# Sums of u in the FFN's first down product, and sums of weights by SP's and POOL's queues

## Chip, cores and metric

The kernel runs on 1 core of one Trainium2 chip. The metric is the device time of one execution in microseconds, the median of three runs. A profile of one execution shows what each engine did: PE (TensorE, matmul) with PEld (its weight loads), DVE (VectorE), ACT (ScalarE), POOL (GpSimd) and SP (SyncE, which here only issues transfers). "Lnnn" is a line of the kernel of the profile.

## What is computed

Two layers of a decoder trunk over 528 positions (16 learned meta tokens and a sequence of 512) with 1024 channels. Each layer has a mixer (attention with forget gates, a Conformer convolution module and a short gated convolution, side by side) and a gated FFN:

```python
def ffn_sublayer(h, pre_g, post_g, w_up, conv_w, w_down):
    u = rms_norm(h, pre_g)
    z = jnp.einsum("bld,df->blf", u, w_up)
    z = causal_depthwise_conv(z, conv_w)          # 3 taps
    g, up = jnp.split(z, 2, axis=-1)
    y = jnp.einsum("blf,fd->bld", jax.nn.silu(g) * up, w_down)
    return h + rms_norm(y, post_g)
```

D_FF is 2816, so there are 22 blocks of 128 gate rows and 22 of up rows. All is float32.

## The kernel before

**Tiling.** Activations lie transposed: 128 channels of a k block on the partitions, 8 such blocks (KD), 528 columns. Weights are laid out by the host in chunks, mostly 128 x 1024 floats (512 KB): one block of output rows with all eight k blocks. A float32 product is made of three matmuls on two-part numbers: every weight chunk is loaded into a `raw` buffer (three of them) by SP, cast by ScalarE into `whi` (L579, L569, L716) and subtracted by VectorE into `wlo` (L580, L570, L720); activations are split alike (`uhi`, `ulo`; `y` for the FFN's gated rows, L2111 and L2112). `mm3` (L764) makes hi x hi, hi x lo and lo x hi.

**FFN.** The 22 blocks run in three parts of 8, 7 and 7 (PARTS). In each part, every block makes a gate and an up product, scales it (L2060), convolves it by three taps (ScalarE L2092, VectorE L2094 twice), applies SiLU and the product (L2104, L2108), and splits it into `y` (L2111, L2112). Then comes that part's down product, over 8 row blocks of output m: 24 matmuls of 512 columns each, the first two row blocks together with the last k of both held to the end. The part's output is copied (part 0, ScalarE L2323) or added (part 1, VectorE L2325) into `yp`. The third part's down product is the stage's end.

**Pairs by seven products.** In layer 1, 12 of the blocks after the first part (SEVEN) use a Strassen-like scheme (`seven_pair`, products L2216): gate and up are the two rows of a 2 x 2 block matrix, the halves of k and of the columns make the rest, and seven half-size products replace eight. It needs two things. First, sums of u: `normalised()` writes u times its gain into `yp` (16 steps `un`, L2149), makes four sums in two halves of k (`total` L2168, `split` L2172 and L2173: 8 steps each), and splits u itself into `uhi` and `ulo` (`block`, L2160 and L2161: four steps, each over a half of k and a half of the columns). Second, sums of the weights: for each of the 12 blocks four tiles of 128 x 512 (U0+U1, U0+G0, U0+U1+G0 and all four of U0, U1, G0, G1, the halves of k of up and gate), in two DRAM tensors `w_sum_c` and `w_sum_b`, later loaded as chunks "c" and "b" beside the plain half "d" (L562).

**Where that work stands.** From block 2 of layer 1's first part on, `build(6)` does up to six steps of `normalised()` after each block's product with SiLU; a `None` in the sequence ends a call; after the last block `build()` does all that is left, ahead of the down product. The sums of weights are made by POOL alone: four plain copies and four accumulating transfers of 256 KB per block, in five steps. `tick` takes steps from a list: it copies one element on POOL, which waits for a row of the work (L2129), and issues the step behind it (L531). Six blocks are done in layer 0's FFN, one step a tick, and six in layer 1's first part, two steps a tick.

**What sets the order.** In the mixers and around the ends of the down products a planner (`Flow`) writes out the order of PE, ACT, DVE and POOL. Everywhere else, and on SP's queue throughout, the order is fixed when the program is built: what is ready and finds its engine free is put next, the earliest in the program first. `tc.issue_after(ins)` puts those instructions of a block that run on the engine of `ins` behind it, and no others. SP issues one transfer at a time and waits in order. In the mixers, `flow.op("sp", ...)` hands a transfer to the planner; its place in the program is then the planner's, but SP is not among the engines whose order is written out.

At the start, SP loads `pv`, the first weights (L712) and h (L492), and then weights as `raw` buffers come free.

## Time and profile before

| | us |
|---|---|
| median of 3 runs (1287.41 to 1289.52) | 1288.8 |
| the profiled execution | 1289.34 |
| its span, first to last instruction | 1287.5 |
| VectorE busy | 888.6 |
| ScalarE busy | 667.1 |
| POOL busy | 201.0 |

The transfers that the change touches, from the profile's list of issues (line, engine, operation, count, size of each, median time from issue to landing):

```profile
w_sum_c<-in_w_dram POOLq DMA_DIRECT2D x36, 256.0 KB, 5.7
w_sum_b<-in_w_dram POOLq DMA_DIRECT2D x36, 256.0 KB, 6.4
raw<-w_sum_c SPq DMA_DIRECT2D x12, 512.0 KB
raw<-w_sum_b SPq DMA_DIRECT2D x12, 512.0 KB
...
w_sum_b<-w_sum_c POOLq DMA_DIRECT2D x12, 256.0 KB, 5.0
...
w_sum_c<-w_sum_b POOLq DMA_DIRECT2D x12, 256.0 KB, 5.2
```

The span covers the first to the last instruction; the execution's own time is 1.84 us longer. A wait is written as "engine, target, line <- releaser"; in a timeline each row has its start, its length, the engine, the line, and in brackets the idle time before it with what ended it. Busy shares of PE are modelled, since matmuls are pipelined. An idle engine costs time only where another, in the end TensorE, waits for it.

### The profile page before, as it was taken

Reading aid. Unit: us, or ns where it says so; the run is one execution under the profiler, and the core shown is the slowest. Engines: PE = TensorE matmul, PEld = TensorE weight load, DVE = VectorE, ACT = ScalarE, POOL = GpSimd, SP = SyncE. Lnnn points to the kernel's source line nnn. Section 1 sums busy time; section 2 is a strip of 40 time slices with the busy share of each in tenths; the row PEclk is TensorE's granted clock in tenths of the full one; section 3 lists DMA queues with packets and bytes.
Section 4 is the critical chain, followed back from the end, with each engine's and each line's share of the span. In section 5 each row is a group of like instructions: output and inputs, shape, how many; then the busy total and the mean of one; then the engine's idle time right before and its main releaser. Section 6 shows DMA issues by size and latency. Waiting matters only on the chain. (4 is left out here: it accounts for less than half of the span.)

```text
span 1287.5 us, 24257 instructions
## 1 busy us (share of the span) xinstructions
PE 1264.1 (98%) x9660; PEld 1209.6 (94%) x9660; DVE 888.6 (69%) x1505; ACT 667.1 (52%) x1273; POOL 201.0 (16%) x406
## 2 busy tenths in 40 slices
PE   8999999999999999999999999999999899999997
PEld 8999899999999999999999998899999689979997
DVE  7888765688644665576588877756799438746864
ACT  7254577564333333244573545766546347626663
POOL 1313311002132013100003133100043330000000
PEclk9999999999999999999999999999999899999999
DMA  7136132504578447523550361334085785434621
GB/s 240 34 101 159 51 100 96 186 18 158 129 243 257 109 130 238 147 83 94 173 196 18 110 167 39 97 130 151 17 213 149 159 248 181 135 123 135 190 73 66
DMA packets 64305, 171.97 MB, mean 134 GB/s; under 512 B 7920, under 2 KB 18288, under 8 KB 64192
## 3 DMA queue, kind: packets, MB, share of 16 engines
q1 hardware_dynamic: 51664, 138.83, 34.1%
q0 software_dynamic: 12528, 31.59, 10.4%
q8 instruction: 76, 1.25, 0.4%
q14 instruction: 37, 0.30, 0.1%
HBM read 148.93 MB, written 35.78 MB: 143 GB/s over the span
## 5 line engine op out<-in xcount | busy, mean ns | idle before, releaser
L764 PE MATMUL psum<-y,whi 128*128 128x264 f32 (+3 forms) x1968 | 386.4, 300 | 5.7 <-ACT y L2111 2.5
L764 PE MATMUL psum<-uhi,whi 128*128 128x264 f32 (+1 forms) x1456 | 349.0, 288 | 1.8 <-ACT uhi L1990 0.8
L764 PE MATMUL psum<-ulo,whi 128*128 128x264 f32 (+1 forms) x1456 | 343.2, 284 | 0.6 <-DVE ulo L1992 0.4
L764 PE MATMUL psum<-uhi,wlo 128*128 128x264 f32 (+1 forms) x1456 | 342.6, 284 | 0.0
L764 PEld LDWEIGHTS psum<-y,whi 128*128 128x128 f32 x1968 | 305.9, 189 | 21.1 <-ACT y L2111 2.9
L764 PE MATMUL psum<-y,wlo 128*128 128x264 f32 (+3 forms) x984 | 273.9, 298 | 0.6 <-DVE wlo L720 0.6
L764 PEld LDWEIGHTS psum<-uhi,whi 128*128 128x128 f32 x1456 | 245.6, 188 | 6.3 <-issue 2.0
L764 PEld LDWEIGHTS psum<-ulo,whi 128*128 128x128 f32 x1456 | 246.0, 188 | 1.3 <-DVE ulo L1992 0.6
L764 PEld LDWEIGHTS psum<-uhi,wlo 128*128 128x128 f32 x1456 | 245.7, 188 | 0.0
L764 PEld LDWEIGHTS psum<-y,wlo 128*128 128x128 f32 x984 | 177.9, 189 | 6.3 <-DVE wlo L720 1.0
L579 ACT CAST whi<-raw 128x1024 fp32r<-128x1024 f32 (+1 forms) x98 | 100.5, 1028 | 160.5 <-PE psum L764 139.2
L580 DVE TENSOR_TENSOR wlo<-raw,whi 128x1024 fp32r<-128x1024 f32 (+1 forms) x98 | 117.1, 1197 | 61.5 <-ACT whi L579 60.5
L2094 DVE SCALAR_TENSOR_TENSOR c<-zs,pv,c 128x528 f32<-128x528 f32 (+1 forms) x176 | 131.6, 756 | 4.7 <-ACT c L2092 2.7
L720 DVE TENSOR_TENSOR wlo<-raw,whi 128x1024 fp32r<-128x1024 f32 (+2 forms) x80 | 95.5, 1204 | 33.1 <-ACT whi L716 32.5
L716 ACT CAST whi<-raw 128x1024 fp32r<-128x1024 f32 (+2 forms) x80 | 81.8, 1030 | 25.4 <-PE psum L764 17.9
L1080 DVE SCALAR_TENSOR_TENSOR cacc<-apad,pv,cacc 128x528 f32<-128x528 f32 x120 | 87.6, 772 | 0.1
L2092 ACT ACTIVATE c<-zs,pv 128x528 f32<-128x528 f32 (+1 forms) x88 | 63.5, 728 | 10.6 <-DVE zs L2254 7.7
L2129 POOL COPY cols<-y 128x1 f32<-128x1 f32 x21 | 18.3, 869 | 303.6 <-ACT y L2111 303.6
L2057 DVE TENSOR_TENSOR zs<-psum,rz 128x528 f32<-128x528 f32 x40 | 28.3, 708 | 53.1 <-PE psum L764 52.1
L2111 ACT CAST y<-c 128x528 fp32r<-128x528 f32 (+1 forms) x44 | 27.6, 628 | 69.4 <-DVE c L2108 69.3
L1535 POOL TENSOR_SCALAR dm<-ident,mcol 128x128 fp32r<-128x128 f32 (+1 forms) x80 | 33.6, 420 | 128.6 <-DVE mcol L1527 127.4
L2104 ACT ACTIVATE c<-c 128x528 f32<-128x528 f32 (+1 forms) x44 | 28.1, 638 | 46.6 <-DVE c L2094 46.6
(265 smaller groups left out, 2039.3 us busy)
## 6 DMA issues: line engine op xcount, KB each, us to landing
raw<-in_w_dram SPq DMA_DIRECT2D x148, 512.0 KB
raw<-in_w_dram SPq DMA_DIRECT2D x32, 448.0 KB
w_sum_c<-in_w_dram POOLq DMA_DIRECT2D x36, 256.0 KB, 5.7
w_sum_b<-in_w_dram POOLq DMA_DIRECT2D x36, 256.0 KB, 6.4
raw<-w_sum_c SPq DMA_DIRECT2D x12, 512.0 KB
raw<-w_sum_b SPq DMA_DIRECT2D x12, 512.0 KB
h<-in_x_dram SPq DMA_DIRECT2D x16, 264.0 KB
raw<-in_w_dram SPq DMA_DIRECT2D x14, 256.0 KB
```

The source lines that it names most:

```text
L579: nc.scalar.copy(hi[:, :sz], raw[:, :sz])
L580: nc.vector.tensor_sub(lo[:, :sz], raw[:, :sz], hi[:, :sz].bitcast(F32))
L716: nc.scalar.copy(box["hi"][:, :sz], box["raw"][:, :sz])
L720: nc.vector.tensor_sub(lo[:, :sz], box["raw"][:, :sz], box["hi"][:, :sz].bitcast(F32))
L764: nc.tensor.matmul(d, lhsT=w[a][:, k, cols], rhs=rhs(b, k, hf), start=start and i == 0 and p == 0, stop=stop and i == n - 1 and p == 2)
L1080: nc.vector.scalar_tensor_tensor(conv[j], in0=src, in1=conv[j], scalar=col("a_dw_w", CK * j + i), op0=ALU.mult, op1=ALU.add)
L1535: diag.append(gp(0.5, lambda qs=qs, end=end, n=n, b=b: nc.gpsimd.tensor_scalar(dm[:n, qs:end], in0=ident[:n, :n], scalar1=mcol[:n, b:b + 1 ...
L2057: nc.vector.tensor_mul(two(t[:, off:]), srcs[0], two(rz))
L2092: nc.scalar.activation(dst, src[:, 2:2 + 2 * fw], AF.Copy, scale=wtap(2, t))
L2094: nc.vector.scalar_tensor_tensor(dst, in0=src[:, i:i + 2 * fw], scalar=wtap(i, t), in1=dst, op0=ALU.mult, op1=ALU.add)
L2104: silu = nc.scalar.activation(cs[0], cs[0], AF.Silu)
L2111: nc.scalar.copy(ghi, cs[0])
```

## The change

Sums of weights: a block now has one DRAM tensor `w_sum` of four tiles. Three plain copies (256, 256 and 512 KB) fill it on SP's queue, and three accumulating transfers (512, 256 and 256 KB) on POOL finish it: four steps a block in place of five, three adds for four. Eight blocks are done in layer 0's FFN by ticks, one step a tick; four in layer 1's mixer, given to the planner 40 us apart with a low priority; none in layer 1's FFN. The loads of "c" and "b" take every second tile, two pieces of 512 floats a partition. The two halves in "b" have changed places, and so the two products with them in `seven_pair`.

Sums of u: `build(5)` runs in blocks 2 to 6 of the first part, and not in block 7. What is left runs in the first down product, after the matmuls of each row block (or of the first two) and up to the next `None`, ahead of the copy into `yp`; on the engine of `glo_ins` (VectorE's last subtraction for `y`, then ScalarE's last copy) it stands behind that instruction. `block(k)` now takes two k blocks over all columns: block(0) in the first slot; the second half's eight sums and block(2) in that of row block 2; block(4) and block(6) in the next two.

```diff
--- before.py
+++ after.py
@@ -31,7 +31,8 @@
 
 SEVEN = (8, 9, 10, 11, 12, 13, 15, 16, 17, 18, 19, 20)
 SEVEN_IN = (1,)
-SUMS = {1: {0: 6, 1: 6}}
+SUMS = {1: (8, 4)}
+SUM_US, SUM_LAT, SUM_EVERY = 0.9, 5.0, 40.0
 K2 = KD // 2
 SB = K2 * P
 AHEAD = 2
@@ -524,16 +525,25 @@
     def sum_steps(l, f):
 
         gate, up = (flat_w(up_chunk[l, t]) for t in (f, NF + f))
-        c, b = sums[l, f] = [T(dram, [P, 2 * SB], F32, f"w_sum_{n}{l}_{f}") for n in "cb"]
-        x, y = slice(0, SB), slice(SB, 2 * SB)
-
-        def put(to, src, add=False):
-            nc.gpsimd.dma_start(to, src, **({"accum_op": ALU.add} if add else {}))
-
-        return [lambda: put(c[:, x], up[:, x]), lambda: put(b[:, y], up[:, x])], \
-            [lambda: put(b[:, x], gate[:, x]), lambda: put(c[:, y], gate[:, y])], \
-            [lambda: put(c[:, x], up[:, y], True), lambda: put(b[:, y], gate[:, x], True)], \
-            [lambda: put(b[:, x], c[:, x], True)], [lambda: put(c[:, y], b[:, x], True)]
+        t = sums[l, f] = T(dram, [P, 4, SB], F32, f"w_sum{l}_{f}")
+        n, o = P * 2 * SB, offs[up_chunk[l, f]]
+        diag = wflat[o:o + 2 * (n + SB)].rearrange("(e q) -> e q", e=2)[:, :n].rearrange("e (p s) -> p e s", p=P)[:, :, :SB]
+
+        def put(to, src):
+            nc.gpsimd.dma_start(to, src, accum_op=ALU.add)
+
+        def copies():
+            nc.sync.dma_start(t[:, 0], up[:, :SB])
+            nc.sync.dma_start(t[:, 1], up[:, :SB])
+            nc.sync.dma_start(t[:, 2:4], gate.rearrange("p (e s) -> p e s", e=2))
+
+        return copies, lambda: put(t[:, 0:2], diag), lambda: put(t[:, 2], t[:, 1]), lambda: put(t[:, 3], t[:, 2])
+
+    def sums_at(l, place):
+
+        counts = SUMS.get(l, ())
+        n0 = sum(counts[:place])
+        return SEVEN[n0:n0 + counts[place]] if place < len(counts) else ()
 
     pw_place = [None]
 
@@ -553,13 +563,14 @@
             return
         if i in seven_up:
             if not parts:
-                c, b = sums[seven_up[i]]
-                parts.extend((("c", c), ("b", b), ("d", flat_w(i)[:, SB:])))
+                t = sums[seven_up[i]]
+                parts.extend((("c", t[:, 1::2]), ("b", t[:, 0:3:2]), ("d", flat_w(i)[:, SB:])))
             kind, src = parts.popleft()
             wpos[0] += not parts
             raw = T(wp, [P, CHUNK], F32, "raw", 3)
-            sz = src.shape[-1]
-            nc.sync.dma_start(raw[:, :sz], src)
+            sz = SB if kind == "d" else 2 * SB
+            nc.sync.dma_start(raw[:, :sz] if kind == "d" else raw[:, :sz].rearrange("p (e s) -> p e s", e=2),
+                              src)
             if kind == "c":
                 hi, lo = (T(tx[0], [P, 2 * SB], F32R, t) for t in ("chi", "clo"))
             elif kind == "b":
@@ -1769,6 +1780,12 @@
                 early.begin(0, PAIRS[0], *pair)
             if over == {"maxima", "fill", "exponentials"}:
                 early.begin(1, PAIRS[1], *banks["st"].slots)
+
+        for i, f in enumerate(sums_at(l, 1)):
+            copies, *adds = sum_steps(l, f)
+            tok = flow.op("sp", 2.0, copies, (Tok(flow.pe + SUM_EVERY * i),), prio=8, lat=SUM_LAT)
+            for op in adds:
+                tok = gp(SUM_US, op, tok, prio=8, lat=SUM_LAT)
 
         for g in (then("maxima", maxima()), att_norms(), then("exponentials", exponentials()), then("fill", fill())):
             flow.thread(g)
@@ -2109,28 +2126,21 @@
                 slot = next(f - sum(PARTS[:p]) for p in range(len(PARTS)) if f < sum(PARTS[:p + 1]))
                 ghi, glo = (t[:, :2 * fw] for t in y_pair(slot))
                 nc.scalar.copy(ghi, cs[0])
-                nc.vector.tensor_sub(glo, cs[0], ghi.bitcast(F32))
+                glo_ins[0] = nc.vector.tensor_sub(glo, cs[0], ghi.bitcast(F32))
                 return ghi, glo
 
             n7 = 2 * ((L - i0 + 3) // 4)
             h7 = [(i0, i0 + n7), (L - n7, L)]
             late_ups = deque()
             seven = SEVEN if l in SEVEN_IN else ()
-            todo = deque()
-            for to, counts in SUMS.items():
-                n0 = sum(counts[x] for x in counts if x < l)
-                fs = [sum_steps(to, f) for f in SEVEN[n0:n0 + counts.get(l, 0)]]
-                for x, y in zip(fs[::2], fs[1::2]):
-                    todo.extend(step for both in zip(x, y) for step in both)
+            todo = deque(step for to, place in ((l + 1, 0), (l, 2)) for f in sums_at(to, place) for step in sum_steps(to, f))
 
             def tick(src):
 
                 if todo:
                     t = nc.gpsimd.tensor_copy(ticks, src.bitcast(F32))
                     with tc.issue_after(t.ins):
-                        for _ in range(1 + l):
-                            for op in todo.popleft():
-                                op()
+                        todo.popleft()()
 
             def normalised():
 
@@ -2153,10 +2163,8 @@
                     k0, (a, z) = b
                     return yp[:, k0:k0 + K2, a:z]
 
-                def block(b):
-                    k0, (a, z) = b
-                    a += skip * (b in (b12, b22))
-                    c = (slice(None), slice(k0, k0 + K2), slice(a, z))
+                def block(k):
+                    c = (slice(None), slice(k, k + 2), slice(i0, L))
                     nc.scalar.copy(uhi[c], yp[c])
                     nc.vector.tensor_sub(ulo[c], yp[c], uhi[c].bitcast(F32))
 
@@ -2176,6 +2184,10 @@
                     for k in range(K2):
                         yield lambda b=b, k=k: un(b, k)
                 for k in range(0, K2, 2):
+                    if k:
+                        yield None
+                        yield lambda: block(0)
+                        yield None
                     yield lambda: total(2, k, lambda: at(b12), lambda: at(b22))
                     yield lambda: split(2, k)
                     yield lambda: total(0, k, lambda: at(b11), lambda: at(b12))
@@ -2184,30 +2196,25 @@
                     yield lambda: total(3, k, lambda: at(b21), lambda: raw[1])
                     yield lambda: split(1, k)
                     yield lambda: split(3, k)
-                yield None
-                for b in blocks:
-                    yield lambda b=b: block(b)
+                for k in range(2, KD, 2):
+                    yield lambda k=k: block(k)
+                    yield None
                 ts.extend((t[:, 0], t[:, 1]) for t in tiles)
 
-            mul_ins = [None]
+            mul_ins, glo_ins = [None], [None]
             ts, n_seven, primed = [], [0], set()
             building = [None]
 
-            def build(n=None):
-
-                while building[0] is not None and (n is None or n > 0):
-                    try:
-                        op = next(building[0])
-                    except StopIteration:
-                        building[0] = None
+            def build(n):
+
+                for op in building[0]:
+                    if op is None:
                         return
-                    if op is None:
-                        if n is not None:
-                            return
-                        continue
                     op()
-                    if n is not None:
-                        n -= 1
+                    n -= 1
+                    if n == 0:
+                        return
+                building[0] = None
 
             def product(bank, w, k0, rhs, start, stop):
 
@@ -2246,13 +2253,13 @@
                 nc.scalar.copy(tmp, bz)
                 finish_pair()
                 wb = next_w()
-                product(y, wb, 0, t(1), False, False)
+                product(y, wb, K2, t(1), False, False)
                 nc.scalar.copy(gate[:, hi], by[:, skip:])
                 product(x, w, K2, u(K2, h7[0]), False, True)
                 nc.scalar.copy(gate[:, lo], bx)
                 product(z, wc, K2, u(K2, h7[1]), False, True)
                 nc.vector.tensor_sub(gate[:, hi], bz[:, skip:], gate[:, hi])
-                product(y, wb, K2, t(2), False, False)
+                product(y, wb, 0, t(2), False, False)
                 nc.scalar.copy(up[:, hi], by[:, skip:])
                 nc.vector.tensor_sub(up[:, hi], up[:, hi], tmp[:, skip:])
                 wd = next_w()
@@ -2295,12 +2302,10 @@
                             continue
                         scaled(i, [ps[:, :, :H]] if i0 == 0 else [ps[:, hf, :iws[hf]] for hf in range(2)])
                     g[f] = ffn_gate(f)
-                    if building[0] is not None:
+                    if building[0] is not None and f < PARTS[0] - 1:
                         with tc.issue_after(mul_ins[0].ins):
-                            build(6)
+                            build(5)
                 finish_pair()
-                if part == 0:
-                    build()
                 ks = list(range(nf))
                 grhs = lambda b, k, hf, f0=f0: g[f0 + k][b][:, fw * hf:fw * (hf + 1)]
                 if part < len(PARTS) - 1:
@@ -2314,20 +2319,23 @@
                                     mm3({0: ps[:, 0, :2 * fw]}, w, group, lambda b, k, hf, f0=f0: g[f0 + k][b][:, :2 * fw], **where)
                                 else:
                                     mm3({hf: ps[:, hf, :fw] for hf in range(2)}, w, group, grhs, **where)
+                        if building[0] is not None:
+                            with tc.issue_after(glo_ins[0].ins):
+                                build(99)
                         for m, ps in zip(some, tiles):
                             if final:
                                 d, src = yp[:, m, t0:], ps[:, 0, :2 * fw]
                             else:
                                 d, src = two(yp[:, m, t0:]), ps[:, :, :fw]
                             if part == 0:
-                                nc.scalar.copy(d, src)
+                                glo_ins[0] = nc.scalar.copy(d, src)
                             else:
                                 nc.vector.tensor_add(d, d, src)
                             if l == 0 and m % 2:
                                 store_one()
                             tick(yp[:, m, t0:t0 + 1])
                 else:
-                    assert not todo
+                    assert not todo and building[0] is None
                     if seven:
                         pools.pop().close()
                         pools.append(ExitStack())
```

## Prediction

> **What bounds the kernel now.** I read the page first, then TensorE's waits, the timeline of TensorE around the longest of them, the windows by stage, and SP's queue. The page:
>
> ```profile
> span 1287.5 us, 24257 instructions
> ...
> PE 1264.1 (98%) x9660; PEld 1209.6 (94%) x9660; DVE 888.6 (69%) x1505; ACT 667.1 (52%) x1273; POOL 201.0 (16%) x406
> ...
> PEclk9999999999999999999999999999999899999999
> ```
>
> TensorE has work in 98% of the span: 23.4 us of idle are all that an edit can take away, plus what a slow clock costs. One slice of 40 (the 32nd) has a lower granted clock. TensorE's waits (total, times, longest), of the whole run:
>
> ```profile
> PE psum L764 <- ACT y L2111: 2.5, 1, 2.5
> PE psum L2216 <- ACT chi L569: 1.6, 1, 1.6
> ...
> PE psum L2216 <- ACT zs L2256: 0.8, 1, 0.8
> ...
> PE psum L1598 <- POOL pf L1578: 0.6, 2, 0.3
> ```
>
> The longest lies at the slow slice: the start of layer 1's first down product, where `build()` empties itself. TensorE's timeline there, and the windows (length, busy of PE, PEld, DVE, ACT, POOL, granted clock, DMA share, GB/s):
>
> ```profile
> 996.49 0.28 PE L2239 MATMUL psum<-uhi,ones_r 128*128 128x258 f32 x1
> ...
> 1002.06 0.40 PE L764 MATMUL psum<-y,wlo 128*128 128x512 f32 x1
> 1004.94 0.74 PE L764 MATMUL psum<-y,whi 128*128 128x512 f32 x2 [2.48 <-ACT y L2111]
> 1006.10 0.79 PE L764 MATMUL psum<-y,whi 128*128 128x512 f32 x1 [0.43 <-DVE y L2112]
> ...
> 1008.56 1.22 PE L764 MATMUL psum<-y,whi 128*128 128x512 f32 x2 [0.38 <-ACT yp L2323]
> ```
>
> ```profile
> 1000.00:1005.00 5.00, 2.52 (x12) 1.72 (x10) 5.00 (x8) 1.84 (x3) 0.00 (x0) 1.00 0.27 103
> 1005.00:1010.00 5.00, 4.19 (x9) 2.56 (x10) 2.79 (x4) 2.96 (x4) 0.70 (x1) 0.59 0.00 0
> 1010.00:1015.00 5.00, 5.00 (x18) 3.95 (x17) 0.71 (x1) 0.00 (x0) 3.59 (x5) 0.73 0.82 197
> ...
> 1020.00:1030.00 10.00, 10.00 (x45) 8.06 (x44) 2.65 (x3) 4.02 (x5) 5.89 (x11) 1.00 0.96 203
> ```
>
> TensorE stands still for 2.48 + 0.43 + 0.38 = 3.3 us, and then works at a clock of 0.59 and 0.73. VectorE is busy for the whole of 1000 to 1005: it is what TensorE waits for. The sums of u are what fills it:
>
> ```profile
> 992.18 2.36 DVE L2161 TENSOR_TENSOR ulo<-yp,uhi 128x1032 fp32r<-128x1032 f32 x2
> ...
> 998.74 2.36 DVE L2161 TENSOR_TENSOR ulo<-yp,uhi 128x1032 fp32r<-128x1032 f32 x2
> 1001.02 0.74 DVE L2094 SCALAR_TENSOR_TENSOR c<-zs,pv,c 128x512 f32<-128x512 f32 x1
> 1001.68 0.69 DVE L2168 TENSOR_TENSOR acc<-yp,acc 128x516 f32<-128x516 f32 x1
> 1002.28 0.74 DVE L2094 SCALAR_TENSOR_TENSOR c<-zs,pv,c 128x512 f32<-128x512 f32 x1
> ...
> 1003.55 0.68 DVE L2108 TENSOR_TENSOR c<-c,c 128x512 f32<-128x512 f32 x1
> ```
>
> The taps of block 7 (L2094) and its product (L2108) stand behind four L2161 and other sums.
>
> **The sums of u.** ScalarE's rows give the whole loss:
>
> ```profile
> 995.96 0.72 ACT L2092 ACTIVATE c<-zs,pv 128x512 f32<-128x512 f32 x1
> ...
> 1004.27 0.62 ACT L2111 CAST y<-c 128x512 fp32r<-128x512 f32 x1
> ...
> 1016.14 1.05 ACT L579 CAST whi<-raw 128x1024 fp32r<-128x1024 f32 x1 [6.20 <-issue]
> ...
> 1021.69 1.05 ACT L579 CAST whi<-raw 128x1024 fp32r<-128x1024 f32 x1 [4.02 <-PE psum L764]
> ```
>
> The cast at 1021.69 starts when row block 3's product frees its buffer, that at 1016.14 one product earlier: a product of 24 matmuls takes 5.55 us, 0.231 us each. Without a stop, the 6 matmuls of the last k and the 24 of block 2 would end 30 x 0.231 = 6.9 us after 1002.46, at 1009.4; they end at 1016.1. So 6.7 us are lost, 3.3 of them idle and 3.4 by the clock. After the change blocks 2 to 6 build five steps each (16 products by the gain and the first 8 sums, 24 in all, where the pause ends the sequence) and block 7 none. Its chain then is ACT L2092 to 996.68, two taps (2 x 0.74), the product 0.68, the cast 0.62: 999.5, and 1000.7 with a weight's subtraction (1.2 us) between: some 2 us before TensorE needs it. What moves: block(0), 8 sums and block(2), block(4), block(6), into the down product, where VectorE is busy for 2.65 of 10 us. The heaviest slot, that of row block 2, has 8 x 0.69 + 1.18 = 6.7 us on VectorE plus a weight's 1.2, against 5.55: the copy of block 2 out of PSUM is late by some 3 us, but TensorE comes back to that bank only a whole product later. The 0.38 for the bank of row block 0 stays. **Term: -6.3 us** (-6.7 to 0; 0 if the sums are again put ahead of block 7).
>
> **The weight sums.** Before: 12 blocks x (4 copies + 4 adds) of 256 KB, all issued by POOL, 6 blocks in each FFN. After: three copies on SP and three adds on POOL a block, 8 blocks in FFN 0 and 4 in mixer 1. POOL's part is lighter and off the path in FFN 0. In layer 1's FFN the transfers vanish that ran beside the loads of the first pairs (chain of waits):
>
> ```profile
> 1038.66 0.24 PE psum L2216 x2
> ...
> 1046.63 5.11 DMA raw<-w_sum_b
> ...
> 1061.29 3.43 DMA raw<-w_sum_b
> ```
>
> With the sums running beside it the load took 5.11, later 3.43. The two waits at L2216 are 2.4 us; against it the new load reads two 2 KB pieces a partition instead of one of 4 KB, of which the trace has no price. Bounds: 0 to -2.4; **I take -1.0**. In mixer 1 twelve adds go on POOL between the attention's work; TensorE waits for POOL 0.6 us in the whole run at L1598, so there is little cover to lose: between -0.5 and +3, **+0.5**.
>
> **The copies on SP's queue.** This is the term that decides. A tick holds back only what goes on POOL's own queue; a copy on SP waits for nothing (it reads the weights, and its target is fresh). The order of such queues is fixed when the program is built: what is ready and finds its queue free goes out. The trace shows how far that reaches: the priming matmul L2239, asked for only in pair 8, whose first products run at 1038.66, ran at 996.49, between the matmuls of the stage before. So I expect the 36 copies (12 blocks of 1 MB) in SP's queue where it first has a gap, at the start of the kernel:
>
> ```profile
> 4.75 2.66 SPq L492 DMA_DIRECT2D h<-in_x_dram  x4
> ...
> 17.64 0.33 SPq L712 DMA_DIRECT2D raw<-in_w_dram  x1
> ```
>
> ```profile
> SPq L492 <- DMA h<-in_x_dram: 0.6, 1, 0.6
> ```
>
> ```profile
> 5.00:10.00 5.00, 4.82 (x36) 4.61 (x36) 3.06 (x7) 3.87 (x9) 0.15 (x1) 1.00 1.05 384
> 10.00:15.00 5.00, 4.62 (x38) 4.41 (x37) 4.90 (x9) 3.94 (x7) 0.00 (x0) 1.00 1.06 381
> ```
>
> ```profile
> 22.10 1.06 ACT L716 CAST whi<-raw 128x1056 fp32r<-128x1056 f32 x1
> ...
> 28.23 0.62 ACT L1990 CAST uhi<-h 128x528 fp32r<-128x528 f32 x1
> ```
>
> SP is free from 7.41 us on; the DMA engines are full up to 15. SP waits for an earlier transfer before it issues a ninth (the 0.6 us row), so I reckon with eight in flight. A copy's price, from windows in FFN 0, where two copies and one load run (the first two), and one load alone (the last):
>
> ```profile
> 303.00:305.00 2.00, 2.00 (x19) 2.00 (x18) 1.32 (x2) 0.61 (x1) 0.28 (x1) 1.00 0.83 268
> 305.00:307.00 2.00, 2.00 (x18) 2.00 (x18) 0.87 (x2) 1.27 (x3) 0.00 (x0) 1.00 0.67 256
> ...
> 309.00:311.00 2.00, 2.00 (x19) 2.00 (x18) 1.27 (x3) 0.63 (x1) 0.00 (x0) 1.00 0.77 262
> ```
>
> ```profile
> q0 software_dynamic: 12528, 31.59, 10.4%
> ```
>
> 2 x (0.83 + 0.67) = 3.0 us for 1 MB, less 2 x 0.77 = 1.54 for the load, leaves 1.46 for 0.5 MB: 2.9 us a MB. The mean of POOL's queue, adds among it, is 0.104 x 1287.5 / 31.59 = 4.24. The load issued at 17.64 finds up to 7 copies in flight (2.4 MB) and, I estimate, 1.3 MB more put through before it: 3.7 x 2.9 = 10.7 us. From some 12 us, when h is through, come three loads (4.6), the copies and the load itself (1.54): it lands near 28.9 and not before 22.1, its cast. ScalarE's order is written out there, and the cast of the next u (28.23) stands behind it; TensorE waits for that cast. So TensorE stops some 6.8 us longer near 31 us, and pays a slow clock after it as above (3.4): **+10.2 us**; between 0 (copies behind the loads) and, at 4.24 a MB, +15.
>
> The Trainium skill's "DMA: Bandwidth & Descriptors", "Queues, rings and completion order", says that a DMA engine takes turns between queues packet by packet and consumes one queue's descriptors in order. It speaks against this move: beside POOL's queue a load shares the engine, behind a copy on its own queue it waits for all of it. The chain rows agree with the sharing (5.11 against 3.43); a load behind SP's copies no row shows.
>
> **Sum:** -6.3 - 1.0 + 0.5 + 10.2 = +3.4, on the profiled execution's 1289.34 us (1.84 around the span): 1292.7. The median of the runs shown is 0.5 below that execution: **1292 us**.
>
> **Rivals.** (1) The copies do no harm, because they are put behind the loads or into gaps such as those after 26 us: then only the gains stand, 1288.8 - 6.8 = 1282. For it: those gaps, and that few loads are urgent; against it: the full DMA windows at the start. It decides from the point where under 0.5 MB stands ahead of the load at 17.64. This is the side of not slower. (2) All 36 copies stand ahead of that load: 12 x 2.9 = 35 us in place of 10.7, 1316. Against it: eight in flight, and loads go first when they are ready. (3) The sums of u are put ahead of block 7's taps as before, by the same freedom (ScalarE's casts of block(0) and VectorE's first sums of the second half aren't tied down): no gain there, 1298. Against it: only two of those sums can start, 1.4 us.
>
> **How the numbers follow.** Forecast 0.50, (1) 0.28, (2) 0.10, (3) 0.12. The forecast's own range is 1285 to 1298. A measurement tells 0.2%, 2.6 us: of the forecast 0.04 falls on faster, 0.18 on the same, 0.28 on slower; of (1) 0.25 faster, 0.03 same; (2) and (3) are slower. Faster 0.29, same 0.21, slower 0.50. The range runs from 1281 to 1303: it takes in (1), the forecast and (3), and leaves out (2) and an edge.
>
> **What would show it.** SP's queue in the first 60 us: copies standing between the loads of L712. TensorE's waits: the 2.5 us at L2111 gone and the clock at 1.00 from 1000 to 1015; a new wait near 31 us for ScalarE's u cast. VectorE near 8 of 10 us in the slot of row block 2. I am wrong if the copies lie elsewhere in SP's queue, or if the wait for L2111 is still there.

## The result, and the profile after

The changed kernel takes 1309.69 us (median of 4 runs, 1308.81 to 1311.29) against 1288.51 (1287.41 to 1289.52) in the same session: 1.0166 times as long, 95% interval 1.0148 to 1.0184. The forecast was 1292 with a range up to 1303: right in its sign and in the place of the largest loss, wrong in its size. The page of the changed kernel (profiled execution 1310.36 us):

```profile
span 1308.4 us, 24186 instructions
...
PE 1267.3 (97%) x9660; PEld 1213.1 (93%) x9660; DVE 889.8 (68%) x1505; ACT 667.2 (51%) x1273; POOL 156.8 (12%) x333
...
PEclk8799999999999999999999999999999999999999
DMA  9913422522359545742461573537032335444521
```

The engines do what they did before (POOL 44 us less). The low clock has gone from the 32nd slice and stands in the first two; there the DMA engines are full. TensorE's waits (total, times, longest):

```profile
PE psum L775 <- ACT uhi L2007: 14.1, 1, 14.1
PE psum L912 <- DVE acc L872: 5.0, 1, 5.0
PE psum L2223 <- ACT chi L580: 2.5, 2, 1.4
PE psum L2223 <- ACT zs L2263: 2.0, 3, 1.3
```

The wait of 2.5 us for block 7's `y` is gone. Two new ones of 19.1 us in all take its place, and the waits of the pairs (L2223) have grown from 2.4 to 4.5 us: before, both lay in the first pairs (1055.60 and 1067.31), now 2.9 us of them lie in the last ones, between 1198 and 1233. SP's queue at the start:

```profile
8.14 0.63 SPq L536 DMA_DIRECT2D w_sum<-in_w_dram  x1
...
11.48 0.35 SPq L723 DMA_DIRECT2D raw<-in_w_dram  x1
...
30.96 0.49 SPq L536 DMA_DIRECT2D w_sum<-in_w_dram  x1
32.57 0.33 SPq L723 DMA_DIRECT2D raw<-in_w_dram  x1
...
53.52 0.49 SPq L538 DMA_DIRECT2D w_sum<-in_w_dram  x1
```

All 36 copies go out between 8.14 and 54 us, whatever their places in the program. Three stand ahead of the first load after h (11.48), 19 ahead of the fourth (32.57): six blocks and one copy of 256 KB, 6.25 MB. The chain of waits says what SP itself waits for (start, length, what):

```profile
12.92 9.31 DMA w_sum<-in_w_dram
...
40.37 9.03 DMA raw<-in_w_dram
```

Each of these transfers needs some 9 us from issue to landing. SP's next transfer goes out at 22.24, when the copy issued at 12.92 has landed, with seven others issued in between: eight are in flight, as the forecast reckoned. A load issued at 40.37, behind 25 copies, takes 9.03 us as well. ScalarE's rows, its idle time and what ended it in brackets:

```profile
41.34 1.07 ACT L727 CAST whi<-raw 128x1056 fp32r<-128x1056 f32 x1 [11.71 <-DMA raw<-in_w_dram]
...
46.19 0.62 ACT L2007 CAST uhi<-h 128x528 fp32r<-128x528 f32 x1
49.42 1.07 ACT L727 CAST whi<-raw 128x1056 fp32r<-128x1056 f32 x1 [2.61 <-DMA raw<-in_w_dram]
50.40 1.16 ACT L2007 CAST uhi<-h 128x528 fp32r<-128x528 f32 x2
```

The cast that the forecast put at 28.9 comes at 41.34 (22.10 before), and a second late one, of the load issued at 40.37, stands at 49.42 between the casts of u. The same casts before:

```profile
28.75 1.07 ACT L716 CAST whi<-raw 128x1056 fp32r<-128x1056 f32 x1
30.33 0.63 ACT L1990 CAST uhi<-h 128x528 fp32r<-128x528 f32 x1 [0.51 <-DVE h L1986]
```

TensorE's first product with u, before and after the change:

```profile
31.02 0.39 PE L764 MATMUL psum<-uhi,whi 128*128 128x264 f32 x1 [0.80 <-ACT uhi L1990]
```

```profile
51.08 0.59 PE L775 MATMUL psum<-uhi,whi 128*128 128x264 f32 x1 [14.08 <-ACT uhi L2007]
```

It follows the second cast of u (begun at 30.33 and 50.40), not the first (28.23 and 46.19), and so it also waits for the weight cast between the two. The windows (length, busy of PE, PEld, DVE, ACT, POOL, granted clock, DMA share, GB/s), of 60 us of the changed kernel:

```profile
0.00:60.00 60.00, 38.72 (x242) 37.07 (x243) 31.60 (x58) 25.66 (x44) 3.71 (x25) 0.80 1.00 330
```

and of the kernel before:

```profile
0.00:60.00 60.00, 56.29 (x429) 55.01 (x430) 47.73 (x87) 30.82 (x56) 15.03 (x51) 1.00 0.44 147
```

TensorE works 17.6 us less in them, with 187 matmuls fewer, and its clock is 0.80 against 1.00. Around the stop, in the changed kernel:

```profile
40.00:45.00 5.00, 0.00 (x0) 0.00 (x0) 2.55 (x5) 3.21 (x7) 0.00 (x0) 0.58 1.06 347
45.00:50.00 5.00, 0.00 (x0) 0.00 (x0) 3.96 (x11) 2.39 (x6) 0.00 (x0) 0.50 1.03 350
50.00:55.00 5.00, 3.77 (x15) 3.47 (x16) 3.94 (x8) 2.83 (x5) 0.00 (x0) 0.50 1.03 357
55.00:60.00 5.00, 5.00 (x33) 5.00 (x32) 5.00 (x11) 1.27 (x2) 0.00 (x0) 0.72 1.01 300
```

The down product of layer 1's first part, on TensorE's timeline and in its windows, shows the other half of the change, which works as foretold:

```profile
1028.58 0.73 PE L775 MATMUL psum<-y,whi 128*128 128x512 f32 x2 [0.97 <-ACT yp L2331]
```

```profile
1015.00:1020.00 5.00, 5.00 (x29) 4.29 (x28) 4.37 (x8) 2.20 (x3) 0.00 (x0) 1.00 0.31 87
...
1030.00:1035.00 5.00, 5.00 (x24) 4.01 (x23) 4.91 (x7) 3.31 (x5) 0.00 (x0) 1.00 0.65 210
1035.00:1040.00 5.00, 5.00 (x23) 4.05 (x22) 3.06 (x3) 2.47 (x5) 0.00 (x0) 1.00 0.33 108
```

No wait for `y` and a clock of 1.00; what is left is the wait for row block 0's bank, 0.97 us instead of 0.38. VectorE is full (4.91 of 5) from 1030 to 1035, in row block 2's slot, 7.97 of 10 us up to 1040 where the forecast named 8, and TensorE doesn't wait for it.

**Where the time went.** ScalarE casts every block's `y` by one line (L2111 before, L2128 after), so these rows mark the same work in each trace. Three of the changed kernel's, the first block of layer 0's FFN, block 7 and the last:

```profile
313.85 0.64 ACT L2128 CAST y<-c 128x528 fp32r<-128x528 f32 x1 [1.26 <-DVE c L2125]
...
1021.56 0.62 ACT L2128 CAST y<-c 128x512 fp32r<-128x512 f32 x1 [3.31 <-DVE c L2125]
...
1260.74 0.62 ACT L2128 CAST y<-c 128x512 fp32r<-128x512 f32 x1 [2.35 <-DVE c L2125]
```

and the same three before (block 7's, 1004.27, stands in the prediction):

```profile
291.09 0.64 ACT L2111 CAST y<-c 128x528 fp32r<-128x528 f32 x1 [1.26 <-DVE c L2108]
...
1239.44 0.62 ACT L2111 CAST y<-c 128x512 fp32r<-128x512 f32 x1 [2.36 <-DVE c L2108]
```

The table gives, for the changed kernel and for each experiment below, by how many us a stretch became longer (+) or shorter (-) than before, from the starts of such casts at its two ends. The ends in the kernel before are 291.09, 612.09, 936.30, 1004.27 (block 7), 1065.70 (first pair) and 1239.44.

| profile | start | FFN 0 | mixer 1 | FFN 1 to block 7 | to first pair | pairs | sum |
|---|---|---|---|---|---|---|---|
| after | +22.8 | +0.7 | +0.3 | -6.5 | +0.1 | +3.9 | +21.3 |
| e1_held | 0.0 | +1.1 | -0.2 | -6.4 | +0.1 | +4.0 | -1.5 |
| e2_pool | -0.3 | +0.9 | +4.6 | -6.5 | +0.1 | +5.4 | +4.3 |
| e3_u_alone | +0.2 | 0.0 | -0.1 | -6.5 | +4.8 | +0.1 | -1.5 |
| e4_whole | +21.9 | +0.3 | +0.4 | -6.4 | -0.3 | +4.3 | +20.1 |
| e6_pool_start | +5.3 | +0.7 | -0.1 | -6.5 | 0.0 | +4.9 | +4.5 |
| e7_four | +11.4 | +0.6 | -0.2 | -6.2 | +0.6 | +5.8 | +12.0 |
| e5_apart | -0.1 | +1.6 | -0.4 | -6.4 | -1.6 | +0.8 | -6.0 |
| e8_old_u | +0.1 | +2.5 | +0.1 | 0.0 | -3.7 | +1.5 | +0.5 |
| e10_gapped | +0.4 | +2.6 | +0.3 | -6.5 | -0.6 | +4.9 | +1.2 |
| e11_stretch | +1.1 | +1.2 | -0.4 | -6.5 | -1.3 | -0.4 | -6.2 |

Each row is one execution; executions of one kernel differ by 2 to 5 us between lowest and highest, so a tenth means little, and medians decide what a kernel takes. Three of these executions lie well above their kernel's median: e8's by 3.0 us (it is the slowest of 12), e7's by 2.5 and e3's by 1.5.

### The profile page after: what moved, and what is told of

Read it like the earlier page. It is cut to its first block, busy times and chain, and to the rows that moved or that the text cites. A ratio compares the mean times of both kernels' runs of the same rounds, so it can differ in the third digit from the quotient of the medians.

```text
span 1308.4 us, 24186 instructions
## 1 busy us (share of the span) xinstructions
PE 1267.3 (97%) x9660; PEld 1213.1 (93%) x9660; DVE 889.8 (68%) x1505; ACT 667.2 (51%) x1273; POOL 156.8 (12%) x333
## 4 chain that ended last, share of the span: by engine, by line
PE 82%; DMA 8%; DVE 5%; ACT 3%; issue 1%; POOL 0%; DVEq 0%; SPq 0%; ACTq 0%
PE psum L775 67%; PE psum L1345 4%; PE psum L1609 3%; DMA raw<-w_sum 3%; DMA raw<-in_w_dram 3%; DMA w_sum<-in_w_dram 2%; PE psum L2223 2%; PE psum L1575 2%; PE psum L912 1%; PE psum L1531 1%; ACT whi L580 1%; PE psum L1675 1%; DVE c L2111 1%; PE psum L1261 1%; DMA h<-in_x_dram 1%
## 5 line engine op out<-in xcount | busy, mean ns | idle before, releaser
L2111 DVE SCALAR_TENSOR_TENSOR c<-zs,pv,c 128x528 f32<-128x528 f32 (+1 forms) x176 | 131.8, 758 | 4.8 <-ACT c L2109 2.7
L2128 ACT CAST y<-c 128x528 fp32r<-128x528 f32 (+1 forms) x44 | 27.6, 628 | 69.3 <-DVE c L2125 69.3
L1575 PE MATMUL psum<-q,k 128*128 128x128 f32 (+2 forms) x192 | 51.2, 348 | 0.3 <-ACT q L1557 0.3
L1609 PE MATMUL psum<-pf,vals 128*128 128x400 f32 (+3 forms) x160 | 50.7, 399 | 0.6 <-POOL pf L1589 0.6
```

Of the source, the lines that this page charges most:

```text
L1575: nc.tensor.matmul(s, lhsT=k[:, ka:ka + kn], rhs=q[:, s0:qz], start=i == 0, stop=i == 1)
L1609: nc.tensor.matmul(acc[:, s0 - qa:qz - qa], lhsT=vals[:, b].rearrange("p h d -> p (h d)")[:, o:o + P], rhs=box["p"], start=b == 0, stop=b ...
L2111: nc.vector.scalar_tensor_tensor(dst, in0=src[:, i:i + 2 * fw], scalar=wtap(i, t), in1=dst, op0=ALU.mult, op1=ALU.add)
```

## Experiments

**e1_held.** Theory: the copies' place in SP's queue costs the time. The rival: the sums' other edits do. The edit puts each group of copies behind the last weight load asked for so far:

```diff
         def copies():
-            nc.sync.dma_start(t[:, 0], up[:, :SB])
-            nc.sync.dma_start(t[:, 1], up[:, :SB])
+            with tc.issue_after(last_load[0].ins):
+                nc.sync.dma_start(t[:, 0], up[:, :SB])
+                nc.sync.dma_start(t[:, 1], up[:, :SB])
...
-            nc.sync.dma_start(raw[:, :sz] if kind == "d" ...
+            last_load[0] = nc.sync.dma_start(raw[:, :sz] if kind == "d" ...
...
```

> The copies stay on SP's queue, but each group of three is put behind the last weight load that the program has asked for by then, so none can move to the start. Theory A (their place in SP's queue costs the 22.8 us that the changed kernel is late by its first 60 us): the start is as before, ScalarE's casts of weights at 15.3 and 22.1 us, no wait of TensorE over 1 us before 60 us; total 1309.7 - 22.8 = 1287 us, and 1284 to 1290 if the copies cost something where they now stand. Theory B (copies on this queue slow the loads wherever they are): the loss moves into the FFN and the mixer, total over 1300 us.

Measured 1288.56 us, ratio 0.9995 (0.9986 to 1.0005). SP's rows:

```profile
9.50 32.65 SPq L725 DMA_DIRECT2D raw<-in_w_dram  x9
...
297.86 0.50 SPq L538 DMA_DIRECT2D w_sum<-in_w_dram  x1
```

Nine loads follow each other at the start, with no copy among them, and 21 us are gone. But the gain of 6.4 us at block 7 didn't reach the end: the pairs give 4.0 back.

**e2_pool.** The same division of the blocks (8 in FFN 0, 4 in mixer 1), with the copies back on POOL:

```diff
         def copies():
-            nc.sync.dma_start(t[:, 0], up[:, :SB])
+            nc.gpsimd.dma_start(t[:, 0], up[:, :SB])
...
```

> The same split of 8 blocks in the first FFN and 4 in the second mixer, but the copies are back on POOL's queue, held by their tick or by the planner's order. Theory A: start as before, total 1287 us, like the run with the copies held on SP's queue, within 2 us. If copies beside loads on one queue cost something of their own, this one is faster than that one by that amount. The planner's order of the second mixer changes by four POOL steps more; within 1 us.

Measured 1293.55, ratio 1.0033 (1.0019 to 1.0047): a miss, since 1287 was expected. The loss is in mixer 1, +4.6, and TensorE's longest wait names part of it, with POOL's row behind which the longest `dm` stands:

```profile
PE psum L1555 <- POOL dm L1546: 3.2, 3, 2.2
```

```profile
758.12 0.84 POOL L533 DMA_DIRECT2D w_sum<-w_sum  x1 [2.08 <-DMA w_sum<-w_sum]
```

POOL waits 2.08 us for one add to land, issues the next, and only then makes the decay `dm` that the attention waits for (2.17 us, at 759.43). With POOL's 12 copies in the mixer its steps stand in another order than in e1. In this mixer TensorE's waits for `dm` are 2.8 us in place of 0.4, and one for `k` of 1.0 is new; the rest of the 4.6 us is not traced to a wait. So moving the copies to SP's queue was worth about 5 us in this mixer (1293.55 - 1288.56), if they are held back.

**e3_u_alone.** The kernel before with the sums of u moved and nothing else:

```diff
-                    if building[0] is not None:
+                    if building[0] is not None and f < PARTS[0] - 1:
                         with tc.issue_after(mul_ins[0].ins):
-                            build(6)
+                            build(5)
                 finish_pair()
-                if part == 0:
-                    build()
...
+                        if building[0] is not None:
+                            with tc.issue_after(glo_ins[0].ins):
+                                build(99)
```

> The kernel before with only the sums of u changed (five steps a block, the rest in the first down product). By the shift of the traces between block 7's products and row block 2 (23.75 to 18.14 us) this part is worth 5.6 us: 1288.5 - 5.6 = 1282.9 us, the 2.5 us wait at block 7's y gone. My forecast for this part was 6.3: 1282.2. Rival: the gain is given back in the pairs, which then wait for their loads sooner (loads bound them): 1285 to 1288 us, with waits at the pairs' products (L2216 before, another number here) of 5 us and more in place of 2.4.

Measured 1286.36, ratio 0.9974 (0.9962 to 0.9986): the time is the rival's. Block 7 comes 6.5 us earlier, the first pair only 1.6 (1064.12 against 1065.70); TensorE's waits in the pairs are 4.1 us, where the rival had 5 and more. The chain of waits there:

```profile
1041.13 6.61 DMA raw<-w_sum_b
...
1050.17 7.03 DMA raw<-in_w_dram
```

These two stood at 5.11 and 4.76 before, issued at 1046.63 and 1054.17. They are issued 5.5 and 4.0 us earlier now, but POOL's sums still run beside them, and they take 1.5 and 2.3 us longer: the second lands only 1.7 us earlier. Without the sums beside them they take 4.18 and 3.49 (e5 below).

**e4_whole.** The changed kernel with its four tiles in another order, so that a load of "c" or "b" reads one piece of 4 KB in a partition's 8 KB instead of two of 2 KB:

```diff
-                parts.extend((("c", t[:, 1::2]), ("b", t[:, 0:3:2]), ("d", flat_w(i)[:, SB:])))
+                parts.extend((("c", t[:, 2:]), ("b", t[:, :2]), ("d", flat_w(i)[:, SB:])))
```

> The changed kernel with its four tiles in another order, so that each load of c and b reads one piece of 4 KB a partition as before (the adds and one copy get the split pieces instead). The copies still run at the start. Theory C (the smaller pieces make the pairs' loads slow): the shift stays near 18 us through the pairs in place of rising from 17.4 to 21.3; total 1306.5 us, 3 below the changed kernel. Rival D (the pairs are late because TensorE comes to them sooner, and loads bound them): no change, 1309.7 us.

Measured 1309.57, ratio 1.0156 (1.0138 to 1.0173): as the changed kernel. The size of the pieces isn't what the pairs lose by (+4.3).

**e6_pool_start.** What of the 22.8 us comes of standing in line, what of the traffic? The changed kernel with its 36 copies on POOL's queue, at the start as well:

```diff
         def copies():
-            nc.sync.dma_start(t[:, 0], up[:, :SB])
...
+            pass
...
+        early_tick = flow.op("pool", 0.7, lambda: nc.gpsimd.tensor_copy(ticks, h[:, 2, L - 1:L]), [h_at[1, 2]])
...
+                nc.gpsimd.dma_start(t[:, 0], up[:, :SB])
+                nc.gpsimd.dma_start(t[:, 1], up[:, :SB])
+                nc.gpsimd.dma_start(t[:, 2:4], gate.rearrange("p (e s) -> p e s", e=2))
...
+            flow.op("pool", 1.6, plain, [early_tick])
```

> The changed kernel, but its 36 plain copies are issued on POOL's queue, all at the start as soon as the third quarter of h's second half has landed (near 10 us). Same bytes at the same time, another queue. Theory A1 (what costs is that a load stands in line behind copies on its own queue): the loads share the engines with the copies, the fourth load after h lands some 5 us late in place of 19, the start is 3 to 8 us late, total 1290 to 1296 us. Theory A2 (what costs is the copies' traffic at that time, on whichever queue): the start is 15 to 23 us late, total over 1302 us. POOL can do nothing else until it has issued them; its next work that others need is near 46 us.

Measured 1294.13, ratio 1.0039 (1.0025 to 1.0054). Its windows and ScalarE's row of the same load:

```profile
0.00:60.00 60.00, 53.57 (x381) 52.40 (x382) 42.29 (x78) 30.42 (x54) 26.14 (x70) 0.94 0.99 338
```

```profile
26.57 1.07 ACT L725 CAST whi<-raw 128x1056 fp32r<-128x1056 f32 x1 [3.94 <-DMA raw<-in_w_dram]
```

The DMA engines are as full as in the changed kernel (0.99 and 338 GB/s against 1.00 and 330), yet the cast comes at 26.57 instead of 41.34 and the start loses 5.3 us instead of 22.8. About three quarters of the loss go with the place in line, and the rest is the traffic. One difference is left: the first copy goes out 6.4 us later here (14.58 against 8.14), so part of the three quarters may be the later start. The Trainium skill's "DMA: Bandwidth & Descriptors", "Queues, rings and completion order", has an engine take turns between queues and take up one queue's descriptors in order. These two traces (26.57 and 41.34) agree with it.

**e7_four.** A dose: FFN 0's copies held as in e1, those of mixer 1's four blocks left free.

```diff
+        def free():
+            nc.sync.dma_start(t[:, 0], up[:, :SB])
+            nc.sync.dma_start(t[:, 1], up[:, :SB])
+            nc.sync.dma_start(t[:, 2:4], gate.rearrange("p (e s) -> p e s", e=2))
+
+        if f in SEVEN[8:]:
+            copies = free
```

> The first FFN's copies held on SP's queue, those of the four blocks of the second mixer free as in the changed kernel: 12 copies, 4 MB, move to the start, all ahead of the fourth load after h (in the changed kernel 19 copies, 6.25 MB, stand ahead of it and it lands at 41.3 us). If the price is that of the changed kernel (41.3 = 12 + 4.6 for three loads + 6.25 MB + 1.5, so 3.7 us a MB): lands at 33, its cast 11 us late, start 14 to 16 us late with the slow clock, total 1303 us. By the price of my forecast, 2.9: lands at 29.7, start 11 us late, total 1299.6 us. If the whole 12 MB matter rather than what stands ahead of that load: a third of 21, total 1295.6 us.

Measured 1298.64, ratio 1.0079 (1.0063 to 1.0094). SP's last rows of the start, and ScalarE's of the fourth load after h:

```profile
24.37 0.49 SPq L545 DMA_DIRECT2D w_sum<-in_w_dram  x1
25.42 27.39 SPq L732 DMA_DIRECT2D raw<-in_w_dram  x6
```

```profile
33.19 1.07 ACT L736 CAST whi<-raw 128x1056 fp32r<-128x1056 f32 x1 [2.89 <-DMA raw<-in_w_dram]
```

With 4 MB ahead the cast is at 33.19, with 6.25 MB at 41.34: 8.15 / 2.25 = 3.6 us a MB, where the forecast took 2.9 (and named 4.24 as the bound). Back to no copy this line gives 33.19 - 4 x 3.6 = 18.8; the forecast's own sum without copies is 12 + 4.6 + 1.5 = 18.1. (Two doses only; without copies the cast stands at 22.10, and ScalarE doesn't wait for it.) The landing is that of the first expectation, 33; the start loses 11.4 us and not 14 to 16, and the total is 1 us below that of the second, 1299.6, by the price of 2.9. So the first had the price right and what follows from a late cast too large.

**e5_apart and e8_old_u.** Why do the pairs lose 4 us? e5 is e1 with c and b as two tensors, each in one stretch of 512 KB, with four copies and four adds a block as in the kernel before; e8 is e5 with the sums of u as before.

```diff
-        t = sums[l, f] = T(dram, [P, 4, SB], F32, f"w_sum{l}_{f}")
+        c, b = sums[l, f] = [T(dram, [P, 2, SB], F32, f"w_sum_{n}{l}_{f}") for n in "cb"]
...
+                nc.sync.dma_start(b[:, 0], up[:, :SB])
+                nc.sync.dma_start(c[:, 0], up[:, :SB])
+                nc.sync.dma_start(b[:, 1], gate[:, :SB])
+                nc.sync.dma_start(c[:, 1], gate[:, SB:])
```

> Copies held on SP's queue as in the run before, and c and b again two tensors, each read as one stretch of 512 KB; for that a block takes four copies and four adds of 256 KB. Theory E (a load of c or b out of the shared tensor, whose rows stand 8 KB apart, takes 5.1 to 5.5 us in place of 4.4 to 4.8, and in the last pairs such a load is what each pair waits for): the shift against the kernel before stays near -4 us through the pairs of the third part in place of rising from -4.1 to -1.5; total 1286 us, 2.5 below the run with copies held. Rival F (the pairs lose it because TensorE is earlier and the loads are bound by something else): no change, 1288.6 us.

> The same with the sums of u as in the kernel before. If the sums of u are worth their full 6.4 us here, 1292.4 us where the other gives 1286; if the pairs give back what they gave back with the sums of u alone (3.6 of 6.4), 1289. The wait of 2.5 us for block 7's y is there again in either case.

e5 measured 1282.30, ratio 0.995 (0.9938 to 0.9962): with e11 the best here, faster than both kernels, and 3.7 us better than expected. e8 measured 1286.71, ratio 0.9985 (0.9976 to 0.9993), less than either value that was expected (1292.4 and 1289). The wait of 2.5 us for block 7's `y` is back. So the sums of u are worth 4.4 us here by the medians; the 6.5 between the two profiles count e8's slow execution. The table suggests that the two edits help each other: between the start of FFN 1 and the first pair, the sums of u alone bring 1.7 us (e3: -6.5 + 4.8), the weights alone 3.7 (e8), and both 8.0 (e5: -6.4 - 1.6).

**e10_gapped and e11_stretch.** e5 changed the layout and the number of transfers at once. e10 is e5 with the two tensors interleaved again; e11 is e1, with its three copies and its adds, with c and b in one stretch each.

```diff
-        c, b = sums[l, f] = [T(dram, [P, 2, SB], F32, f"w_sum_{n}{l}_{f}") for n in "cb"]
+        t = T(dram, [P, 4, SB], F32, f"w_sum{l}_{f}")
+        c, b = sums[l, f] = t[:, 1::2], t[:, 0::2]
```

```diff
-        t = sums[l, f] = T(dram, [P, 4, SB], F32, f"w_sum{l}_{f}")
+        t = sums[l, f] = T(dram, [2, P, 2 * SB], F32, f"w_sum{l}_{f}")
```

> The kernel with held copies and the sums of c and b in two tensors (1282.3 us), with one edit: the two sums lie in one tensor with their halves interleaved, as in the changed kernel; its four copies and four adds a block stay. If the layout is what the pairs lose by, they lose some 4 us between the first and the last pair again (the layer's last pair stands 4 us later against the first than in the kernel before) and the time is 1286 to 1289; if the number and size of the copies and adds is what counts, the time stays at 1282.3 and the pairs lose 1 us or less.

> The kernel with held copies (1288.56 us: three copies and two-tile adds a block) with one edit: c and b each lie in one stretch of memory; copies and adds keep their number and size. If the layout is what the pairs lose by: 1282 to 1284, and the pairs lose 1 us or less between the first and the last; if the number and size of the copies and adds is what counts: 1286 to 1289 and the pairs lose 4 us.

e10: 1289.68, ratio 1.0003 (0.9994 to 1.0012). e11: 1282.92, ratio 0.995 (0.9937 to 0.9962). It is the layout. The chain of waits of e10 in the last pairs:

```profile
1193.92 5.65 DMA raw<-w_sum
...
1205.58 5.12 DMA raw<-w_sum
```

and of e11:

```profile
1177.58 4.39 DMA raw<-w_sum
...
1188.01 4.52 DMA raw<-w_sum
```

The last four loads of this kind in the two chains are 4.44, 5.47, 5.65 and 5.12 us in e10 and 3.44, 4.39, 4.52 and 4.40 in e11. So a load of 512 KB from every second part of a stretch of 1 MB takes about 1 us longer here than the same 512 KB in one piece, and in the pairs some of it is waited for.

## Why the prediction was right or wrong

**The copies on SP's queue: +10.2 forecast, +22.8 measured. This step failed.** Right were where the copies go, that eight transfers are in flight, that the load of 17.64 stands behind copies, and that TensorE then waits for a cast of u and runs at a slow clock. Wrong was "The load issued at 17.64 finds up to 7 copies in flight (2.4 MB) and, I estimate, 1.3 MB more put through before it". It counted the copies by the clock of the trace before, up to 17.64. But SP's order is fixed when the program is built, and in it 19 copies stand ahead of that load (in e7 all twelve that were free). SP works through them in order and waits for earlier ones to land, so the load wasn't issued at 17.64 but at 32.57, behind 6.25 MB. Of the 12.4 us between 28.9 and 41.3, (6.25 - 3.7) x 2.9 = 7.4 are this number of copies and 6.25 x 0.7 = 4.4 their price. A second late load came on top. The forecast had TensorE wait for the cast of u at 28.23; it waits for the next one (30.33), and the weight cast between them (28.75) belongs to one more load, which went out at 40.37. TensorE takes up u at 51.08 in place of 31.02, 20.1 us late: 18.0 come with the first cast of u (46.19 - 28.23), 2.1 with the load behind it (the second cast follows the first by 4.2 us in place of 2.1). The other 2.7 of the 22.8 are the slow clock after the stop. The forecast had 6.8 and 3.4 for the two. Rival (2), all 36 copies ahead, was off the other way, though nearer (1316): 17 of them went behind that load. Rival (1), copies that do no harm, fell; e1 shows what it takes to make it true.

**The sums of u: -6.3 forecast, -6.5 measured at block 7,** and -6.2 to -6.5 in the ten profiles of kernels with that edit. Block 7's wait is gone, the clock stays at 1.00, row block 2's slot is full, without a wait of TensorE. Rival (3) fell. What the step left out is what comes late next: by itself (e3) 4.8 of the 6.5 us are lost again at the first pair, whose loads run beside the sums of weights. Only since the other edit takes those sums away does the gain last.

**The weight sums in the pairs: -1.0 forecast, +4.0 measured.** Two effects lie in it, each larger than thought. The bound of 2.4 was the sum of two waits as they stand before the change. By itself that held: in e8 the first pair comes 3.7 us earlier, and 2.2 are left at the last. But with the sums of u moved TensorE comes sooner, and the loads hold it up more: e3 loses 4.9 us in these two stretches and e11 gains 1.7, so that there the edit, with each load in one stretch, is worth 6.6. Against it, the interleaved layout costs 5.8 (0.1 + 4.0 in e1, -1.3 - 0.4 in e11). The forecast's terms were added as if each stood alone; which one the +4.0 is booked under depends on the order. From e3 (+4.9) to the changed kernel (+4.0) it is -0.9, close to the -1.0 only because two errors nearly cancel. The forecast named the layout as an operation without a price, but its bounds (0 to -2.4) left no room for a loss. It suspected the 2 KB pieces; e4 shows that pieces of 4 KB, 8 KB apart, lose as much.

**Mixer 1: +0.5 forecast, +0.3 measured.** **FFN 0: nothing forecast, +0.7 measured,** and up to +2.6 where the copies run in it.

**Sum.** By the forecast's terms +3.4; by the profiles +22.8 + 0.7 + 0.3 - 6.5 + 0.1 + 3.9 = +21.3, against 21.2 between the medians. With 22.8 for the first term the forecast would have been 1305, so that step holds 12.6 us of the miss of 17.9 (21.3 - 3.4), and the pairs 5.0.

**Open.** Why 512 KB in every second piece lands later than 512 KB in one stretch isn't shown; a layout with another distance wasn't tried. The spread of FFN 0 between the held kernels (+1.1 to +2.6) was not traced to a wait.

## What to carry to other kernels

A transfer that waits for nothing goes out where its queue first has a gap, and everything later on that queue stands behind it: count what stands ahead of the next urgent load by the program's order, not by the times of the old trace, or tie the transfer to a load (`issue_after` on the same engine), which here was worth 21 us. Keep what one load reads in one stretch, also when it is only passed through DRAM; this was worth 5.6 us here by the medians from e1 to e11, and 6.8 by the ratios from e10 to e5. An earlier engine gains only as much as the next load allows: look at which transfers run beside that load before a gain is added up.

## What was not expected of the hardware

- A copy inside DRAM on SP's queue delayed the load behind it by 3.6 us a MB (33.19 to 41.34 from 4 to 6.25 MB), more than the 2.9 from windows in which copies on POOL's queue shared the engines. The same 12 MB on POOL's queue, with the DMA engines as full but the first copy 6.4 us later, delayed that load's cast by 4.5 us (22.10 to 26.57) in place of 19.2.
- The last three 512 KB loads from interleaved DRAM took 5.1 to 5.7 us in e10, those from one stretch 4.4 to 4.5 in e11 (though one of e5's took 5.42 and one of e8's 5.16), with pieces of 2 KB and of 4 KB alike by what the pairs lost (+4.9 and +3.9 in e10 and after, +4.3 in e4).
- The granted clock stood at 0.50 for two windows, the second of them with TensorE at work again for 3.77 of 5 us, and at 0.72 in the next (40 to 60 us above). After the stop of 14.08 us the matmuls of 264 columns start 0.22 us apart up to 57.70, for 6.6 us, and 0.12 us apart from there on. The Trainium skill's "TensorE: Matmul & The Clock Gate", "What's actually happening", has half the clock after some 3.4 us without work, and the full clock after some 3.4 us of sustained work. The half clock here agrees with it; the return took longer than that. The stop of 2.48 us before the change (0.43 close behind it) is shorter than that time, and still the clock fell, between 1005 and 1006 (0.93 there, 0.50 in the next us); there the measurement decides.
